# A hybrid encoder block on one core: where the constants are loaded, when the first half's squares are made, and 24 products of the output projection placed elsewhere

## The chip, the core and the metric

The kernel runs on one core of a Trainium2 chip. The metric is the device time of one execution in microseconds (us), as the median of several executions. The engines are named as in the profile: PE (TensorE, matrix products), DVE (VectorE), ACT (ScalarE), POOL (GpSimd), SP (SyncE, which issues most transfers). A "product" is one PE instruction of 128x128 weights by 128x512 columns.

## What is computed

One layer of an encoder block on x of 1024 positions by 1024 channels, in float32: a mixing part (a short gated convolution on one half of the channels, a gated 31-tap convolution with a layernorm on the other) and a gated MLP. Cut to the part of the program that the change touches:

```python
h   = rmsnorm(x, norm_mix_g)
z   = h @ w_in                       # 1024 -> 2560: a_h, a_bg, a_cg, b_val, b_gate, 512 each
y_a = a_bg * dwconv(a_cg * a_h, conv_a_w)                 # 3 taps
u   = dwconv(b_val * sigmoid(b_gate), conv_b_w) + conv_b_b  # 31 taps
y_b = silu(layernorm(u, ln_b_g, ln_b_b))
x   = x + concat(y_a, y_b) @ w_out
# then: h = rmsnorm(x); x = x + (silu(dwconv3(h @ w_gate)) * (h @ w_up)) @ w_down; final rmsnorm
```

## The kernel before

Channels lie on the partitions, positions along the free dimension, in two halves of 512 positions (h = 0 and 1). Each float32 operand of a product is split into a high part (a rounded copy) and a low part (the rest): a tile's k-th step is three products, high x high, high weights x low, low weights x high. ACT makes high parts and DVE or POOL the low ones by a subtraction (`minus`, L93, called from `split`, L131).

**The start (L200 to L282).** The first two tiles of the input projection (gate and value of group 0, weights `w01`) are made step by step as data arrive: `load_h1` makes the high part of x times the norm's gain on ACT (L213) and the low part on DVE (L214), both need the constants `cst`; `split_w01` splits the weights in three pieces, k = 0 to 1, 2 to 3, and 4 to 7 (a copy on DVE, L245, then the subtraction, L93). Each k has six products (L271): 48 of half 0, then 48 of half 1. `sq_h1` makes the squares for the RMS norm: ACT squares (L221, L224), and POOL adds them into `acc1[0]` and the first of half 1 into `acc1[1]`; DVE adds the others of half 1 (L226). `stat_h1` sums an accumulator over the partitions on PE (`total_of`, L185 with the high part and L186 with the low part, which DVE writes as `st`, L93); then follow a square root on ACT (L193) and a reciprocal on DVE (L194). After the two tiles the third begins (`mm_tile`, L166).

x comes in by SP's queue, the weights `w01` by ACT's queue (L241), and the constants by POOL's queue (L251).

**The output projection (L394 to L406 and the loop at the end of the printed code).** It runs over the halves; its operands are eight blocks per half: `yA` (4 blocks, from the gated short convolution, L353 to L367) and `yB` (4 blocks, out of `layernorm`, L374 to L387). For half 0 the first four output tiles (`HEAD`) have their products with k = 0, 1, 2 placed ahead of the layernorm's operands. The last product group of the short convolution, j = 3, ends with L366, which frees its pair of PSUM banks. PSUM tiles of products are taken in pairs from a ring (`psum()`).

A scheduler puts the instructions of each engine in order; the products of the first two tiles stand in the order written, and what is written within `urgent()` is preferred. Each engine then runs its own list strictly in order.

Of the kernel before, what the change touches and what calls it, by code (L numbers as in the profile page):

```python
# [9 lines left out]
AF = mybir.ActivationFunctionType  # L10
# [7 lines left out]
KD = D // P  # L18
D_A = 512
NJ = D_A // P  # L20
# [25 lines left out]
def block_kernel(ctx: ExitStack, tc, xT, win01, win, wout, wgate, wup, wdown, consts, outT):  # L46
    nc = tc.nc
# [56 lines left out]
    def psum():  # L104
        return [ps.tile([P, H], F32, tag="mm", name="mm") for _ in range(2)]
# [112 lines left out]
    def sq_h1(h, k):  # L218
        x = xs[h][:, k, :]
        if k == 0:  # L220
            nc.scalar.activation(acc1[h], x, AF.Square)  # L221
        else:
            sq = scratch("sq")
            nc.scalar.activation(sq[:, :H], x, AF.Square)  # L224
            eng = nc.gpsimd if h == 0 or k < 3 else nc.vector
            eng.tensor_tensor(out=acc1[h], in0=acc1[h], in1=sq[:, :H], op=ALU.add)  # L226
# [13 lines left out]
    def load_w01(a, b):  # L240
        nc.scalar.dma_start(raw01[:, a:b], win01[:, a:b])  # L241

    def split_w01(a, b):
        for i, (hi, lo) in enumerate(w01):
            nc.vector.tensor_copy(hi[:, a:b, :], raw01[:, a:b, i, :])  # L245
            minus(nc.vector, lo[:, a:b, :], raw01[:, a:b, i, :], f32(hi[:, a:b, :]))

    cuts = ((0, 2), (2, 4), (4, 8))
    nc.sync.dma_start(xs[0][:, 0, :], xT[0, :, 0])
    load_w01(*cuts[0])  # L250
    nc.gpsimd.dma_start(cst, consts)  # L251
    nc.sync.dma_start(xs[0][:, 1, :], xT[0, :, 1])
    load_w01(*cuts[1])
    nc.sync.dma_start(xs[0][:, 2:4, :], xT[0, :, 2:4])
# [6 lines left out]
    with tc.manual_schedule(engines={nc.tensor.engine}):  # L261
        for h in range(2):
            for k in range(KD):
                load_h1(h, k)
                if h == 0:
                    for a, b in cuts:
                        if k == a:
                            split_w01(a, b)
                for wz, xz in ((0, 0), (0, 1), (1, 0)):
                    for pt, w in zip((pg, pv), w01):  # L270
                        nc.tensor.matmul(pt[h], w[wz][:, k, :], a1(h, k)[xz], start=k + wz + xz == 0, stop=k == KD - 1 and wz == 1)  # L271
                sq_h1(h, k)
                if h == 1 and k == 3:
                    with urgent():
                        stat_h1(0)

        def late_stat(k):
            if k == 5:
                with urgent():
                    stat_h1(1)  # L280

        pg1 = mm_tile(2, a1, late_stat)  # L282
# [87 lines left out]
    def layernorm(h):  # L370
        cc = [half(cb[j], h) for j in range(NJ)]
        s, std = half(ub[2 * h], 0), half(ub[2 * h], 1)
        q, r = half(ub[2 * h + 1], 0), half(ub[2 * h + 1], 1)
        nc.vector.tensor_tensor(out=s, in0=cc[0], in1=cc[1], op=ALU.add)  # L374
        nc.vector.tensor_tensor(out=s, in0=s, in1=cc[2], op=ALU.add)
        nc.vector.tensor_tensor(out=s, in0=s, in1=cc[3], op=ALU.add)
        m = total(s, nc.vector)
        for j in range(NJ):
            nc.vector.scalar_tensor_tensor(cc[j], m, -1.0 / D_A, cc[j], ALU.mult, ALU.add)
            nc.scalar.activation(q if j == 0 else s, cc[j], AF.Square)  # L380
            if j:
                nc.vector.tensor_tensor(out=q, in0=q, in1=s, op=ALU.add)
        rstd(total(q, nc.vector), std, r, eps_l, D_A)
        for j in range(NJ):
            nc.vector.tensor_tensor(out=cc[j], in0=cc[j], in1=r, op=ALU.mult)
            nc.scalar.activation(cc[j], cc[j], AF.Silu, scale=col(LN_G + j), bias=col(LN_B + j))
            split(cc[j], yB[h][:, j, :], yB[h][:, NJ + j, :], nc.vector)  # L387
# [6 lines left out]
    def out_mm(pt, e, w, h, ks):  # L394
        for k in ks:
            mm3(half(pt, e), w[0][:, k, :], w[1][:, k, :], *y_of(h, k), k == 0, k == KD - 1)
# [45 lines left out]
    for h in range(2):  # L442
        pts, ws = {}, {}

        def start(dt):
            ws[dt] = get(N_IN + 8 * h + dt, 0 if h == 0 and dt < HEAD else 2)
            if dt % 2 == 0:
                pts[dt // 2] = psum()

        head = HEAD if h == 0 else 0  # L450
        for dt in range(head):
            start(dt)
            out_mm(pts[dt // 2], dt % 2, ws[dt], h, range(NJ - 1))
        if h == 0:
            with urgent():
                layernorm(0)
            layernorm(1)
        for dt in range(KD):
            nc.sync.dma_start(half(xr[dt], h), xT[h, :, dt])
            if dt >= head:  # L460
                start(dt)
            out_mm(pts[dt // 2], dt % 2, ws[dt], h, range(NJ - 1 if dt < head else 0, KD))
            out_done(pts[dt // 2], dt, h, accs2[h])
            if h == 1 and dt == 1:
                stat_r2(0, accs2[0])
                norm_x(0, range(KD))
                to_op("B11", 0, 0)
                to_op("B21", 4, 0)
# [675 lines left out]
```

## Time and profile before

| what | value |
|---|---|
| median of 3 runs | 1011.09 us (1010.94 to 1011.56) |
| the profiled execution, its own time | 1009.84 us |
| its span in the trace | 1008.1 us |
| mean granted PE clock | 0.989 of full speed |
| PE busy | 968.3 us, 96% of the span |
| DVE busy | 746.6 us, 74% |
| ACT busy | 446.3 us, 44% |
| POOL busy | 443.8 us, 44% |

The span is the time from the first to the last instruction that the profile records; 1.7 us of the execution lie outside. The profiled execution was 1.25 us faster than the median. All times in the rows below are counted from the start of the span. "Idle before <-X" is time in which the engine stood still ahead of the row, and X is what released it.

### The profile page before, as it was taken

How to read it: one execution, taken by the hardware profiler on the slowest of the kernel's cores; microseconds unless marked ns; L12 is line 12 of the kernel's file. 1: busy time of each engine (PE TensorE's matmuls, PEld its weight loads, DVE VectorE, ACT ScalarE, POOL GpSimd, SP SyncE). 2: the span in 40 equal slices, each digit the busy share in tenths (PEclk: the TensorE clock that was granted, in tenths of full speed). 3: DMA queues.
4: the chain of work that ended last, by engine and by line, in shares of the span. 5: the costliest groups of instructions: out<-in, count | busy, mean ns of one | idle time of the engine just before them, and what ended most of it. 6: DMA issues, size and time to landing. Idle time of an engine off the chain costs nothing.

```text
span 1008.1 us, 11577 instructions
## 1 busy us (share of the span) xinstructions
PE 968.3 (96%) x4202; PEld 792.6 (79%) x4202; DVE 746.6 (74%) x891; ACT 446.3 (44%) x623; POOL 443.8 (44%) x304
## 2 busy tenths in 40 slices
PE   6999999998999999899999999999998999999993
PEld 4888888886888887788888888888786788888883
DVE  7899999999678797754654654654559798786557
ACT  7354421234564456434443443443446353534352
POOL 4189853344853006345244344344325534342006
PEclk8999999999999999999999999999999999999997
DMA  6211111123563204133134133223284763544104
GB/s 255 84 43 63 42 43 62 42 63 105 178 219 128 82 1 149 71 117 135 63 106 145 63 105 132 77 104 120 88 270 140 239 192 98 181 126 125 43 1 167
DMA packets 63178, 112.56 MB, mean 112 GB/s; under 512 B 5488, under 2 KB 26992, under 8 KB 62864
## 3 DMA queue, kind: packets, MB, share of 16 engines
q1 hardware_dynamic: 62640, 110.65, 32.9%
q10 hardware_dynamic: 432, 1.05, 0.3%
q8 instruction: 33, 0.54, 0.2%
q14 instruction: 25, 0.20, 0.1%
q0 software_dynamic: 48, 0.12, 0.0%
HBM read 84.79 MB, written 27.00 MB: 111 GB/s over the span
## 4 chain that ended last, share of the span: by engine, by line
PE 85%; DVE 6%; issue 3%; DMA 2%; POOL 2%; ACT 1%; SPq 0%; POOLq 0%; DVEq 0%; ACTq 0%
PE a L546 28%; PE mm L166 19%; PE c L546 13%; PE b L546 8%; PE mm L152 3%; PE mm L154 3%; PE mm L153 3%; PE a L681 2%; PE mm L271 2%; PE c L681 1%; DMA xd<-x2d 1%; DVE wlo L93 1%; PE y L154 1%; PE y L153 1%; PE y L152 1%
## 5 line engine op out<-in xcount | busy, mean ns | idle before, releaser
L166 PE MATMUL mm<-r,whi 128*128 128x512 f32 x576 | 155.3, 389 | 0.0
L546 PE MATMUL a<-r,whi 128*128 128x512 f32 x472 | 147.4, 393 | 5.9 <-ACT a L531 5.0
L315 DVE SCALAR_TENSOR_TENSOR cv<-u,cst,cv 128x512 f32<-128x512 f32 x203 | 138.9, 749 | 0.7
L166 PEld LDWEIGHTS mm<-r,whi 128*128 128x128 f32 x576 | 108.1, 188 | 22.4
L546 PE MATMUL c<-r,whi 128*128 128x512 f32 x392 | 120.7, 389 | 0.0
L93 POOL TENSOR_TENSOR wlo<-raw,whi 128x1024 fp32r<-128x1024 f32 x30 | 76.7, 2556 | 81.3 <-ACT whi L131 81.1
L131 ACT ACTIVATE whi<-raw 128x1024 fp32r<-128x1024 f32 (+1 forms) x68 | 69.2, 1019 | 95.6 <-PE mm L166 32.9
L546 PEld LDWEIGHTS a<-r,whi 128*128 128x128 f32 x472 | 89.1, 189 | 26.7 <-ACT a L531 5.8
L500 POOL TENSOR_TENSOR s<-raw,s 128x512 f32<-128x512 f32 (+1 forms) x31 | 40.1, 1292 | 139.6 <-DVE wlo L93 118.4
L500 POOL TENSOR_TENSOR s<-up 128x512 f32<-128x512 f32 (+1 forms) x31 | 42.1, 1358 | 133.9 <-DMA up<-wup 117.1
L546 PE MATMUL a<-r,wlo 128*128 128x512 f32 x236 | 93.0, 394 | 2.3 <-DVE wlo L93 2.3
L166 PE MATMUL mm<-r,wlo 128*128 128x512 f32 x288 | 90.2, 389 | 0.0
L131 ACT ACTIVATE whi<-s 128x1024 fp32r<-128x1024 f32 (+1 forms) x52 | 52.2, 1004 | 77.2 <-POOL s L500 59.3
L546 PEld LDWEIGHTS c<-r,whi 128*128 128x128 f32 x392 | 73.6, 188 | 15.3
L93 DVE TENSOR_TENSOR wlo<-s,whi 128x1024 fp32r<-128x1024 f32 (+1 forms) x52 | 65.0, 1249 | 27.7 <-ACT whi L131 27.7
L90 POOL TENSOR_TENSOR t<-t 128x512 f32<-128x512 f32 x36 | 53.8, 1506 | 66.7 <-DVE t L603 66.7
L624 DVE TENSOR_TENSOR t<-a,c 128x512 f32<-128x512 f32 x40 | 27.4, 686 | 69.9 <-issue 37.3
L546 PE MATMUL c<-r,wlo 128*128 128x512 f32 x196 | 76.2, 389 | 0.0
L531 ACT ACTIVATE a<-a 128x512 f32<-128x512 f32 x76 | 45.1, 593 | 65.2 <-PE a L546 62.5
L546 PE MATMUL a<-r,ahi 128*128 128x512 f32 x224 | 70.5, 396 | 1.1 <-DVE xd L862 1.1
L546 PE MATMUL b<-r,whi 128*128 128x512 f32 x232 | 71.4, 389 | 0.0
L131 ACT ACTIVATE r<-r 128x512 fp32r<-128x512 f32 x71 | 43.7, 628 | 52.4 <-DMA r<-ydT 23.6
(209 smaller groups left out, 2114.9 us busy)
## 6 DMA issues: line engine op xcount, KB each, us to landing
raw<-wgate SPq DMA_DIRECT2D x22, 512.0 KB, 4.7
up<-wup SPq DMA_DIRECT2D x20, 512.0 KB, 3.3
raw<-win SPq DMA_DIRECT2D x18, 512.0 KB, 3.3
ydT<-t SPq DMA_DIRECT2D x36, 256.0 KB, 2.0
r<-ydT SPq DMA_DIRECT2D x36, 256.0 KB, 3.3
raw<-wout SPq DMA_DIRECT2D x16, 512.0 KB, 3.4
ydB<-t SPq DMA_DIRECT2D x27, 256.0 KB, 2.0
r<-ydB SPq DMA_DIRECT2D x27, 256.0 KB, 4.4
```

The source lines that it names most:

```text
L90: nc.gpsimd.tensor_tensor(out=out, in0=a, in1=b, op=op)
L93: eng.tensor_tensor(out=out, in0=a, in1=b, op=ALU.subtract)
L131: nc.scalar.activation(hi, y, AF.Copy)
L152: nc.tensor.matmul(out, whi, hi, start=first, stop=False)
L153: nc.tensor.matmul(out, whi, lo, start=False, stop=False)
L154: nc.tensor.matmul(out, wlo, hi, start=False, stop=last)
L166: nc.tensor.matmul(outs[h], w, a[h][z], start=s0, stop=s1)
L315: nc.vector.scalar_tensor_tensor(fin if k == KC - 1 else acc, src, w, acc, ALU.mult, ALU.add)
L500: self.eng.tensor_tensor(out=self.t[:, i * self.w : (i + 1) * self.w], in0=a, in1=b, op=op)
L531: nc.scalar.activation(t, b, AF.Copy)
L546: nc.tensor.matmul(out, w[wz][:, k, :], x[xz], start=first and k + wz + xz == 0, stop=k == n - 1 and wz == 1, skip_group_check=not first)
L681: nc.tensor.matmul(out, w[wz][:, k, :], xz, start=first and k == 0 and wz == 0 and xz is hi, stop=not first and k == 3 and wz == 1)
```

## The change

The constants' transfer goes from POOL's queue to the head of ACT's queue, ahead of the weights. The high parts of the third piece of `w01` (k = 4 to 7) are made by ACT instead of DVE. The squares of half 0 are issued four steps later, the last four during half 1, and the first total stands after k = 5 of half 1 instead of k = 3. In the output projection the four head tiles' products of k = 3 and twelve products of half 1's first output tile (with half 0's weights, into a pair of banks `first1`) are written ahead of the loop over the output tiles.

```diff
@@ -242,13 +242,16 @@
 
     def split_w01(a, b):
         for i, (hi, lo) in enumerate(w01):
-            nc.vector.tensor_copy(hi[:, a:b, :], raw01[:, a:b, i, :])
+            if a < 4:
+                nc.vector.tensor_copy(hi[:, a:b, :], raw01[:, a:b, i, :])
+            else:
+                nc.scalar.activation(hi[:, a:b, :], raw01[:, a:b, i, :], AF.Copy)
             minus(nc.vector, lo[:, a:b, :], raw01[:, a:b, i, :], f32(hi[:, a:b, :]))
 
     cuts = ((0, 2), (2, 4), (4, 8))
     nc.sync.dma_start(xs[0][:, 0, :], xT[0, :, 0])
+    nc.scalar.dma_start(cst, consts)
     load_w01(*cuts[0])
-    nc.gpsimd.dma_start(cst, consts)
     nc.sync.dma_start(xs[0][:, 1, :], xT[0, :, 1])
     load_w01(*cuts[1])
     nc.sync.dma_start(xs[0][:, 2:4, :], xT[0, :, 2:4])
@@ -269,8 +272,13 @@
                 for wz, xz in ((0, 0), (0, 1), (1, 0)):
                     for pt, w in zip((pg, pv), w01):
                         nc.tensor.matmul(pt[h], w[wz][:, k, :], a1(h, k)[xz], start=k + wz + xz == 0, stop=k == KD - 1 and wz == 1)
-                sq_h1(h, k)
-                if h == 1 and k == 3:
+                if h == 0 and k >= 4:
+                    sq_h1(0, k - 4)
+                if h == 1:
+                    if k < 4:
+                        sq_h1(0, k + 4)
+                    sq_h1(1, k)
+                if h == 1 and k == 5:
                     with urgent():
                         stat_h1(0)
 
@@ -444,10 +452,12 @@
 
         def start(dt):
             ws[dt] = get(N_IN + 8 * h + dt, 0 if h == 0 and dt < HEAD else 2)
-            if dt % 2 == 0:
+            if dt % 2 == 0 and dt // 2 not in pts:
                 pts[dt // 2] = psum()
 
         head = HEAD if h == 0 else 0
+        if h == 1:
+            pts[0] = first1
         for dt in range(head):
             start(dt)
             out_mm(pts[dt // 2], dt % 2, ws[dt], h, range(NJ - 1))
@@ -455,11 +465,15 @@
             with urgent():
                 layernorm(0)
             layernorm(1)
+            for dt in range(head):
+                out_mm(pts[dt // 2], dt % 2, ws[dt], h, [NJ - 1])
+            first1 = psum()
+            out_mm(first1, 0, ws[0], 1, range(NJ))
         for dt in range(KD):
             nc.sync.dma_start(half(xr[dt], h), xT[h, :, dt])
             if dt >= head:
                 start(dt)
-            out_mm(pts[dt // 2], dt % 2, ws[dt], h, range(NJ - 1 if dt < head else 0, KD))
+            out_mm(pts[dt // 2], dt % 2, ws[dt], h, range(NJ if dt < head or (h, dt) == (1, 0) else 0, KD))
             out_done(pts[dt // 2], dt, h, accs2[h])
             if h == 1 and dt == 1:
                 stat_r2(0, accs2[0])
```

DVE's list from the third piece of the weights to the first reciprocal. r_95 and r_97 are the low parts of x of half 0 and half 1, acc_118 and acc_119 the two halves' accumulators, whi_120 and whi_122 the high parts of `w01`. Before:

```order
L245 CAST whi_120<-rr 128x512
L245 CAST whi_122<-rr 128x512
L214 SCALAR_TENSOR_TENSOR r_95<-c,cst,r_94 128x512
L93 TENSOR_TENSOR wlo_121<-rr,whi_120 128x512
L93 TENSOR_TENSOR wlo_123<-rr,whi_122 128x512
L214 SCALAR_TENSOR_TENSOR r_95<-c,cst,r_94 128x512 x4
L214 SCALAR_TENSOR_TENSOR r_97<-u,cst,r_96 128x512 x4
L226 TENSOR_TENSOR acc_119<-acc_119,sq 128x512
L93 TENSOR_TENSOR st<-acc_118,st 128x512
L214 SCALAR_TENSOR_TENSOR r_97<-u,cst,r_96 128x512 x4
L93 TENSOR_TENSOR wlo<-raw,whi 128x1024 x2
L194 RECIPROCAL rr<-std 128x512
```

And with the change:

```order
L214 SCALAR_TENSOR_TENSOR r_95<-c,cst,r_94 128x512 x4
L93 TENSOR_TENSOR wlo_121<-rr,whi_120 128x512
L93 TENSOR_TENSOR wlo_123<-rr,whi_122 128x512
L214 SCALAR_TENSOR_TENSOR r_95<-c,cst,r_94 128x512 x2
L214 SCALAR_TENSOR_TENSOR r_97<-u,cst,r_96 128x512 x4
L226 TENSOR_TENSOR acc_119<-acc_119,sq 128x512
L214 SCALAR_TENSOR_TENSOR r_97<-u,cst,r_96 128x512 x4
L226 TENSOR_TENSOR acc_119<-acc_119,sq 128x512
L93 TENSOR_TENSOR wlo<-raw,whi 128x1024
L226 TENSOR_TENSOR acc_119<-acc_119,sq 128x512
L93 TENSOR_TENSOR wlo<-raw,whi 128x1024
L93 TENSOR_TENSOR st<-acc_118,st 128x512
```

The two copies are gone, the low parts of x for k = 2 to 5 stand in one row ahead of the weights' third piece, and `st` of the first total has moved from behind one addition to behind three additions, four low parts and two splits of 128x1024 weights (the second and third input tiles' weights come from `raw`).

POOL's list at the start, before:

```order
L251 DMA cst<-consts 128x238
L300 MEMSET u 128x16
L226 ISA
L226 TENSOR_TENSOR acc_118<-acc_118,sq 128x512 x7
L299 MEMSET u 128x16
L226 TENSOR_TENSOR acc_119<-acc_119,sq 128x512 x2
```

And with the change:

```order
L308 MEMSET u 128x16
L226 ISA
L226 TENSOR_TENSOR acc_118<-acc_118,sq 128x512 x5
L307 MEMSET u 128x16
L226 TENSOR_TENSOR acc_119<-acc_119,sq 128x512
L226 TENSOR_TENSOR acc_118<-acc_118,sq 128x512
L226 TENSOR_TENSOR acc_119<-acc_119,sq 128x512
L307 MEMSET u 128x16
L226 TENSOR_TENSOR acc_118<-acc_118,sq 128x512
```

Two of half 0's seven additions now stand behind the MEMSET, which writes into the region of `u` that holds half 1's x and so follows DVE's low part of half 1's k = 0.

PE's list where the output projection begins. r4_98 is yA of half 0, r5_99 yA of half 1; mm_1801, mm_1802, mm_1827 and mm_1828 are the four head tiles, whi_1667 the first head tile's weights, mm_1953 the new pair `first1`. Numbers at the waits are semaphores. Before:

```order
L152 MATMUL mm_1828<-r4_98,whi_1840 128x512 [waits DVE_49,Activation_49]
L153 MATMUL mm_1828<-r4_98,whi_1840 128x512
L152 MATMUL mm_1801<-r4_98,whi_1667 128x512 [waits Activation_49]
L152 MATMUL mm_1802<-r4_98,whi_1730 128x512
L152 MATMUL mm_1827<-r4_98,whi_1823 128x512
L154 MATMUL mm_1828<-r4_98,wlo_1841 128x512 [waits Pool_49]
```

And with the change:

```order
L152 MATMUL mm_1828<-r4_98,whi_1840 128x512 [waits DVE_49,Activation_49]
L153 MATMUL mm_1828<-r4_98,whi_1840 128x512
L152 MATMUL mm_1953<-r5_99,whi_1667 128x512 [waits DVE_49]
L153 MATMUL mm_1953<-r5_99,whi_1667 128x512
L154 MATMUL mm_1953<-r5_99,wlo_1668 128x512
```

These three rows of mm_1953 are its k = 0; six more for k = 1 and 2 follow, and only then the row of mm_1801 that waits for ACT. So nine products have come between the last product that runs before PE's wait and the product that waits. The first of the nine waits for DVE, which frees the pair of banks of the short convolution's last product group in L366.

## Rows read from the trace of the kernel before

**Rows 1.** The page: the span, its first part (busy time, share and instructions of each engine), and the shares of the chain of work that ended last, by engine.

```profile
span 1008.1 us, 11577 instructions
...
PE 968.3 (96%) x4202; PEld 792.6 (79%) x4202; DVE 746.6 (74%) x891; ACT 446.3 (44%) x623; POOL 443.8 (44%) x304
...
PE 85%; DVE 6%; issue 3%; DMA 2%; POOL 2%; ACT 1%; SPq 0%; POOLq 0%; DVEq 0%; ACTq 0%
```

**Rows 2.** What PE waited for from 0 to 420 us: line, releaser, us in total, times, longest.

```profile
PE mm L271 <- DVE r L214: 4.3, 3, 2.9
PE mm L152 <- ACT r L131: 3.5, 1, 3.5
PE a L546 <- ACT a L531: 3.1, 1, 3.1
PE mm L271 <- ACT r L213: 2.8, 1, 2.8
```

**Rows 3.** The chain of work that ended last, pieces in order of time: start, us, what.

```profile
1.26 6.18 DMA cst<-consts
...
47.86 163.23 PE mm L166 x720
...
245.94 0.64 ACT r L131
246.62 0.98 PE mm L152 x3
```

**Rows 4.** Transfers issued in the first 30 us: queue, count, KB each, median us from issue to landing.

```profile
rr<-win ACTq DMA_DIRECT2D x2, 256.0 KB, 5.0
...
cst<-consts POOLq DMA_DIRECT2D x1, 119.0 KB, 6.2
```

**Rows 5.** ACT at the start, two rows: start, us, line, operation, idle before and its releaser.

```profile
5.07 0.63 ACT L221 ACTIVATE acc<-c 128x512 f32<-128x512 f32 x1 [2.38 <-DMA c<-xT]
...
9.70 0.72 ACT L213 ACTIVATE r<-c,cst 128x512 fp32r<-128x512 f32 x1 [0.38 <-DMA c<-xT]
```

**Rows 6.** DVE from 9 to 35 us, start and us of each group of instructions.

```profile
12.81 1.77 DVE L214 SCALAR_TENSOR_TENSOR r<-c,cst,r 128x512 fp32r<-128x512 f32 x1
14.50 2.93 DVE L245 CAST whi<-rr 128x512 fp32r<-128x512 f32 x2
17.36 1.75 DVE L214 SCALAR_TENSOR_TENSOR r<-c,cst,r 128x512 fp32r<-128x512 f32 x1
19.03 2.37 DVE L93 TENSOR_TENSOR wlo<-rr,whi 128x512 fp32r<-128x512 f32 x2
21.33 2.73 DVE L214 SCALAR_TENSOR_TENSOR r<-c,cst,r 128x512 fp32r<-128x512 f32 x4
...
29.30 0.68 DVE L93 TENSOR_TENSOR st<-acc,st 128x512 fp32r<-128x512 f32 x1
...
32.56 2.34 DVE L93 TENSOR_TENSOR wlo<-raw,whi 128x1024 fp32r<-128x1024 f32 x2
```

**Rows 7.** POOL's additions of squares at the start.

```profile
9.40 10.85 POOL L226 TENSOR_TENSOR acc<-acc,sq 128x512 f32<-128x512 f32 x7 [7.31 <-ACT sq L224]
...
24.89 3.34 POOL L226 TENSOR_TENSOR acc<-acc,sq 128x512 f32<-128x512 f32 x2
```

**Rows 8.** PE from 19 to 40 us: the last two waits of the start, the second product of the first total, and the start of the third tile.

```profile
19.16 0.82 PE L271 MATMUL mm<-r,whi 128*128 128x512 f32 x2 [2.88 <-DVE r L214]
...
22.12 1.16 PE L271 MATMUL mm<-r,whi 128*128 128x512 f32 x2 [0.43 <-DVE r L214]
...
33.37 0.39 PE L186 MATMUL total<-st,ones_r 128*128 128x512 f32 x1
...
39.06 1.07 PE L166 MATMUL mm<-r,whi 128*128 128x512 f32 x4
```

**Rows 9.** DVE's reciprocal for the second half's norm.

```profile
48.68 3.35 DVE L194 RECIPROCAL rr<-std 128x512 f32<-128x512 f32 x1 [2.65 <-ACT std L193]
```

**Rows 10.** Stretches of the span: from:to, us, busy time (instructions) of PE, PEld, DVE, ACT and POOL, the granted PE clock (1.00 is the full 2.4 GHz, 0.50 is 1.2 GHz), DMA share, GB/s.

```profile
19.70:23.00 3.30, 2.87 (x7) 1.77 (x6) 3.30 (x5) 3.30 (x7) 0.56 (x1) 0.50 0.00 0
23.10:240.00 216.90, 216.90 (x957) 179.49 (x956) 206.07 (x286) 84.16 (x113) 121.33 (x77) 1.00 0.18 58
241.50:248.30 6.80, 3.30 (x15) 2.41 (x14) 6.73 (x8) 1.23 (x2) 4.25 (x3) 1.00 0.46 137
...
408.80:412.10 3.30, 3.30 (x10) 2.52 (x9) 3.26 (x2) 0.00 (x0) 2.49 (x2) 0.50 0.00 0
```

**Rows 11.** PE behind its wait at 405 us: the first row after it, and the tenth product.

```profile
408.35 0.87 PE L546 MATMUL a<-r,whi 128*128 128x512 f32 x2 [3.12 <-ACT a L531]
...
412.01 0.71 PE L546 MATMUL a<-r,whi 128*128 128x512 f32 x2
```

**Rows 12.** DVE where the output projection begins: the last two low parts of yB of half 0, and the first half's product of the short convolution's last group.

```profile
239.63 5.01 DVE L93 TENSOR_TENSOR r<-c,r 128x512 fp32r<-128x512 f32 x2
...
245.22 0.68 DVE L366 TENSOR_TENSOR y<-mm,y 128x512 f32<-128x512 f32 x1
```

**Rows 13.** The same stretch on POOL: a split of the output projection's weights.

```profile
241.28 2.82 POOL L93 TENSOR_TENSOR wlo<-raw,whi 128x1024 fp32r<-128x1024 f32 x1
```

**Rows 14.** DVE's last low part of yB of half 1, and PE's products that read it.

```profile
287.53 2.29 DVE L93 TENSOR_TENSOR r<-c,r 128x512 fp32r<-128x512 f32 x1
...
290.62 0.62 PE L153 MATMUL mm<-r,whi 128*128 128x512 f32 x2
```

## The prediction

> **What bounds the kernel now.** I began with the page. PE is busy for 96% of the span, and 85% of the chain that ended last is PE's own work [rows 1]. No product is removed by the change, so it can only save time in which PE stands still or runs at half clock. The view of PE's waits lists where that is in the first 420 us, the stretch that the change touches: 4.3 us for low parts of x that DVE makes at the start, 2.8 us for the first high part, 3.5 us once in the output projection, and 3.1 us at 405 us, which the change doesn't touch [rows 2]. The chain names the sources: at the very start the constants, which land 6.18 us after their issue, and at 246 us ACT's high part of the short convolution's output [rows 3]. Last I looked at what lies between the two places. From the end of the start to 240 us PE works without a pause at full clock [rows 10], 720 products in 163.23 us [rows 3], so one product costs 0.2267 us. DVE waits there for what PE produces (its reciprocal at 48.68 us stood 2.65 us idle for a total that PE had to reach) [rows 9]. Therefore PE's start carries through: each microsecond by which the third tile begins earlier than at 39.06 us [rows 8] is worth a microsecond at the end, as long as nothing later takes it back.
>
> **The constants.** Before, they land at 7.44 us [rows 3] and the first high part on ACT follows. At the head of ACT's queue they should land near 5 us, as the weights issued there do, 5.0 us after their issue [rows 4]; the weights go out one issue later. PE may so begin 2 us earlier. I count this as nothing: the third step needs x for k = 2, whose transfer lands when ACT takes it at 9.70 us, after an idle time for that transfer [rows 5]. That is unchanged, so both orders restart there. The same cover hides a later landing too; if x for k = 2 came at once, the 2 us would count in full.
>
> **The start on DVE.** Before, the low part of k = 2 begins only at 12.81 us, since four DVE instructions ahead of it share the time with POOL's additions. The rows show what that costs: POOL's seven additions run from 9.40 to 20.25 us, 1.55 each [rows 7], and in that stretch a low part takes 1.75 to 1.77 us, a copy 1.47, while from 21.33 us four low parts take 2.73, 0.68 each [rows 6]. Each DVE instruction waits for the addition in flight; I call that a hold, and one costs 1.75 - 0.68 = about 1.05 us.
>
> I laid the new lists out by hand with these durations. The second piece of the weights is split before k = 2 arrives. Its high part ends at 10.4, so DVE makes k = 2 at 10.5, k = 3 at 11.1, k = 4 at 12.8 and, held, k = 5 from 13.5 to 15.3. The two copies of the third piece take ACT 0.63 each [rows 5], done at 15.5, ahead of their use. DVE's two subtractions of that piece are both held by POOL's fourth and fifth additions: they end at 17.0 and 18.7. Before they ended at 19.03 + 2.37 = 21.40, and PE's last wait of the start ended at 22.12 [rows 8]. The low part at 18.7 is the operand of product 30 of the 96. From there to the third tile are 67 products and the two of the total, 69 x 0.2267 = 15.6 us: 34.3 instead of 39.06. That alone would be 4.8 us, and it is the upper bound of this term.
>
> **The wait that comes instead.** The second product of the first total (L186) needs the low part `st` on DVE. Before, `st` was made at 29.30 us [rows 6] and PE came to it at 33.37 [rows 8], 3.4 us later. Now both sides move against each other. PE comes 55 products after 18.7, near 31.4. On DVE, k = 6, 7 and half 1's k = 0 end at 20.7; then POOL's list is free to go past its MEMSET and makes three additions in turn, at 1.67 each [rows 7], to 25.9. Half 1's k = 1 ends at 21.3, k = 2 and 3, held, at 24.7; the first addition of DVE's own stands behind POOL's third and ends at 26.6; k = 4, held by POOL's last addition, ends at 28.3; k = 5 to 7 at 30.3; the second addition at 30.9; the first split of 1024 columns (1.17 each [rows 6]) at 32.0; the third addition at 32.7; the second split at 33.9; and `st`, 0.68, at 34.5. So PE waits near 3.1 us, to 34.6. Twelve products and L186 follow, 13 x 0.2267 = 2.95: the third tile begins at 37.55. **First term: 39.06 - 37.55 = 1.5 us faster.** One hold more makes it 0.45, two make it -0.6; with no wait left it is 4.8. I keep 1.5, since the holds that I count are those of the rows.
>
> Late next is the square root and the reciprocal behind the total: they come 1.3 us later than before (34.6 against 33.37), but what reads the first norm is the gate of tile one, which has the third tile (48 products, 10.9 us) as cover. POOL's squares of half 1 and DVE's remaining work are hidden under the same.
>
> **PE's clock.** A wait of that length may cost more. In the kernel before, the wait of 2.88 us that ended at 19.16 [rows 8] is followed by 3.30 us at granted clock 0.50, and the one of 3.12 us that ended at 408.35 too [rows 10, 11]; the wait of 3.50 us in the output projection [rows 2] is not: the clock stays 1.00 [rows 10]. What a fall costs can be read at 408.35: the tenth product began at 412.01, nine products in 3.66 us instead of 2.04, so 1.6 us. The Trainium skill says the same of the cause (TensorE: Matmul & The Clock Gate, section "What's actually happening"): "the default state is throttled, and activity releases the throttle". By that rule a new wait endangers the gain; if the fall were certain and whole, this kernel's sum would be 1.5 + 0.65 - 1.6 = 0.55 us; the trace agrees in two of the three waits of this length. I take that it falls, since two of three did, and that a third of the slow stretch lies still under the wait or beside it: **second term: 1.05 us slower**, bounds 0 and 1.6.
>
> **The output projection.** Before, PE runs out of products with operands at 243.1 and starts again at 246.62, when ACT has made the first high part of the last group's product, which DVE forms in L366 from 245.22 to 245.90 [rows 3, 12]. The change puts nine products into that gap, 9 x 0.2267 = 2.04 us. But the bank pair that they write is freed by that same L366: they wait for DVE until 245.90, and can begin near 245.97 instead of 246.62. **Third term: 0.65 us faster**, not 2.04. The upper bound is 2.04, if the pair were free; the lower is nothing. The other moved products (k = 3, and three of half 1 that have to wait for the second half's high part) change places with others that had their operands: yB's low parts end at 239.63 + 5.01 = 244.64 [rows 12], before PE's restart, so no wait is there to fill. Holding the bank pair of half 1's tile early costs nothing, as the pair was idle. The splits of the weights for the later output tiles come nearer to their use, by those 24 products (24 x 0.2267 = 5.4 us): one split on POOL takes 2.82 [rows 13], so without that cover each would cost up to 2.8; I see about 5 us of cover left and count nothing.
>
> **Sum:** 1.5 - 1.05 + 0.65 = 1.1 us. The profiled execution took 1009.84 us; minus 1.1 is 1008.7, and as it was 1.25 below the median, I expect a median of 1010.0 us. A measurement of this kernel can tell about 0.2%, 2.0 us, from no change.
>
> **The rivals.**
>
> *No fall of the clock, or one hold fewer.* The third wait before left the clock at 1.00. Then the gain is 1.5 + 0.65 = 2.15, with a hold fewer up to 3.6: 1007.5 to 1008.95. Against it stand the two falls. Chance 0.23.
>
> *No wait at the total.* If POOL's additions hold DVE far less in the new order, `st` is ready when PE comes: 4.8 + 0.65 = 5.45, 1005.6. Against it: three splits and additions stand ahead of `st` whatever the holds do. Chance 0.08.
>
> *The gain is eaten whole.* With two holds more, or if half 0's last two additions come still later, the first total takes all, and the output projection stays as it was: -0.6 to 0.5 of gain, 1010.6 to 1011.7. The change then doesn't do what it seems to. Chance 0.14.
>
> *Slower, by a new wait at the end of half 1's layernorm.* DVE's last low part of yB ends at 287.53 + 2.29 = 289.82 and PE's products that read it begin at 290.62 and 290.84 [rows 14], a slack of 1.0. With nine products done earlier PE comes 0.65 sooner relative to DVE, and I see 0.4 of slack left. It decides from 0.4 on: if one split of POOL's (up to 2.82 [rows 13]) holds that chain, PE stalls by 2.0, giving 1.1 - 2.0, so 1012.0; with a fall of the clock behind it, 1.6 more: 1013.6. For it speaks that the 2.29 us of that row is a held instruction already; against it that POOL's list is unchanged there. Chance 0.12.
>
> **How the numbers follow.** The forecast case holds 0.43, with times of 1009 to 1010.9, its likeliest 1010.0. Faster by over 0.2% means below 1009.07: the first two rivals, 0.31, and the forecast's fast edge, 0.06. Slower by over 0.2% is above 1013.1: the last rival's worse part and a rest, 0.08. Between is 0.55. The range that leaves out no more than 0.2 reaches from 1007.0 (leaving out most of the second rival) to 1012.5 (leaving out the clock's fall in the last).
>
> **What the profile of the changed kernel would show.** The first step is right if the third piece's subtractions end near 18.7 us and no wait over 2 us stands at L274 after 10 us. The second: a PE wait of 2 to 4 us at L186 for DVE's `st`, and the third tile near 37.5. The third: a stretch of granted clock 0.50 right after it, or not. The fourth: in the output projection a wait that ends with DVE's product (L374), and nine products of half 1 straight behind it, at 245.97 less the start's net gain. The prediction is wrong if `st` comes before PE, if the clock is other than taken, if the pair is free earlier, or if a wait near 290 us appears that was not there.

## The result and the profile after

The changed kernel took 1014.28 us (median of 6 runs, 1012.92 to 1015.58) where the kernel before took 1011.33 beside it: ratio 1.0028, interval 1.0015 to 1.0041. It is 3 us slower; 1010.0 was forecast. Ratios, here and below, are of executions in the fast state: one execution of e1, 1394.68 us at a mean granted clock of 0.654, is left out of its ratio. The profiled execution took 1012.92 us, 3.1 more than the profiled one of before.

The page of after, lines of its first and fourth part, against [rows 1]:

```profile
span 1011.1 us, 11583 instructions
...
PE 970.1 (96%) x4202; PEld 792.2 (78%) x4202; DVE 746.4 (74%) x889; ACT 447.2 (44%) x625; POOL 441.3 (44%) x303
...
PE 80%; DVE 6%; issue 3%; ACT 3%; DMA 2%; POOL 2%; SPq 0%; POOLq 0%; DVEq 0%; ACTq 0%
```

The work is the same; the chain holds 80% of PE's own work instead of 85%, and 3% of ACT's instead of 1%. What PE waited for from 0 to 420 us in after (line, releaser, us in total, times, longest), against [rows 2]:

```profile
PE total L186 <- DVE st L93: 4.3, 2, 2.8
...
PE mm L152 <- DVE y L374: 2.8, 1, 2.8
...
PE mm L274 <- DVE r L214: 1.7, 2, 1.0
...
PE mm L274 <- DVE whi L246: 1.4, 1, 1.4
PE mm L153 <- DVE r L93: 0.8, 2, 0.6
PE mm L274 <- DVE wlo L93: 0.5, 1, 0.5
```

The 4.3 us for low parts of x at the start shrank to 1.7, the 2.8 us ahead of the first product to 1.4 (it now waits for the weights' copy, L246), and the 3.5 us in the output projection to 2.8. New are 0.5 us for the weights' third piece, the total's second product, once at the start (2.8) and once much later (1.5), and L153, products that read yB.

PE at three places: the last wait of the start, the total and the third tile (against [rows 8]), and the restart in the output projection.

```profile
18.45 1.10 PE L274 MATMUL mm<-r,wlo 128*128 128x512 f32 x2 [0.53 <-DVE wlo L93]
...
34.84 0.50 PE L186 MATMUL total<-st,ones_r 128*128 128x512 f32 x1 [2.77 <-DVE st L93]
...
37.91 1.07 PE L166 MATMUL mm<-r,whi 128*128 128x512 f32 x4
...
244.77 0.79 PE L152 MATMUL mm<-r,whi 128*128 128x512 f32 x1 [2.80 <-DVE y L374]
```

Third tile: 37.91 against 39.06, 1.15 us earlier. Restart: 244.77 against 246.62, 1.85 earlier, so the output projection's wait gave 0.70. But the first product of the feed-forward part (36 products with the norm's operands) begins at 331.98 in after and at 328.74 in before: between these places 5.09 us were lost. Two stretches hold them. First the clock: stretches from:to with PE's busy time (products), PEld, DVE, ACT, POOL, the granted clock, DMA share and GB/s, behind the wait at the total and behind the restart:

```profile
34.80:38.20 3.40, 3.36 (x15) 2.80 (x16) 2.04 (x1) 2.50 (x4) 0.11 (x1) 1.00 0.64 180
...
244.80:248.10 3.30, 3.30 (x8) 2.62 (x9) 3.19 (x5) 1.17 (x2) 2.52 (x2) 0.50 0.62 227
```

Behind the total nothing fell; behind the restart the clock was at half, and the ninth product began at 248.25, 3.48 us after the first, against 1.97 in before (248.59 - 246.62): 1.5 us lost. Then the waits between 285 and 305 us, where before has none:

```profile
290.56 0.50 PE L153 MATMUL mm<-r,whi 128*128 128x512 f32 x1 [0.58 <-DVE r L93]
...
292.25 0.50 PE L153 MATMUL mm<-r,whi 128*128 128x512 f32 x1 [0.27 <-DVE r L93]
...
301.47 0.50 PE L186 MATMUL total<-st,ones_r 128*128 128x512 f32 x1 [1.53 <-DVE st L93]
```

The view counts 2.4 us there, and the starts of neighbouring products 3.1. The whole stretch from the ninth product to the feed-forward part takes 331.98 - 248.25 = 83.73 in after and 328.74 - 248.59 = 80.15 in before, 3.6 more. Sum: -1.15 - 0.70 + 1.5 + 3.6 = +3.25 us.

That is the sum of one pair of executions, and the clock's 1.5 us in it is not to be charged to the change. Three kernels below have the output projection of before (e1, e5 and the one called total last), and in all three the clock fell behind the same restart: from 243 to 252 us it is 0.81, 0.81 and 0.65, against 0.81 in after and 1.00 in before. So the profile of before is the odd one. Against e1, whose clock fell as in after, the stretch from the third tile to the feed-forward part is 294.07 - 291.14 = 2.9 us longer: that is what the moved products cost, the 0.70 that they gained taken off.

Why those waits? ACT's high part of the next weights waits for PE to free a weight buffer. The row in before, then in after:

```profile
252.43 1.06 ACT L131 ACTIVATE whi<-raw 128x1024 fp32r<-128x1024 f32 x1 [5.27 <-PE mm L153]
```

```profile
256.17 1.06 ACT L131 ACTIVATE whi<-raw 128x1024 fp32r<-128x1024 f32 x1 [4.85 <-PE mm L153]
```

Counted from the third tile this is 213.4 before and 218.3 after, 4.9 us later. The order of PE's products says why: the last product that reads the first head tile's high weights was number 53 of the output projection and is now number 71, since the moved products stand ahead of it. 18 x 0.2267 = 4.1, plus the clock's 1.5, less the 0.70 of the earlier restart: 4.9.

The later splits are late with it, by 4.4 to 7.0 us up to the ninth. The layernorm of half 1 is not late from its beginning: the first DVE instruction behind its first total (`c<-total`) begins 221.0 us behind the third tile in after and 220.8 in before. PE finishes its second total 1.9 us late (235.5 against 233.6), and the square root behind that total is 4.4 us late (238.0 against 233.6): in both lists it stands behind the fifth split on ACT. That split and the root in before, then in after:

```profile
268.58 1.04 ACT L131 ACTIVATE whi<-raw 128x1024 fp32r<-128x1024 f32 x1
...
272.68 0.69 ACT L193 ACTIVATE u<-total,eps_l 128x512 f32<-128x512 f32 x1 [0.40 <-PE total L186]
```

```profile
273.05 1.06 ACT L131 ACTIVATE whi<-raw 128x1024 fp32r<-128x1024 f32 x1 [2.85 <-DMA raw<-wout]
...
275.94 0.69 ACT L193 ACTIVATE u<-total,eps_l 128x512 f32<-128x512 f32 x1
```

Before, ACT waits for PE's total. In after PE has the total done at 273.44, while ACT is still at the split, whose weights came late. DVE's last low part of yB then ends 254.3 us behind the third tile instead of 250.8. The wait at the third total has another last link. SP, ACT and DVE in after:

```profile
286.56 5.99 SPq L473 DMA_DIRECT2D c<-xT  x3
292.64 0.38 SPq L127 DMA_DIRECT2D raw<-wout  x1
```

```profile
297.34 1.06 ACT L131 ACTIVATE whi<-raw 128x1024 fp32r<-128x1024 f32 x1 [3.88 <-DMA raw<-wout]
298.31 0.61 ACT L179 ACTIVATE st<-acc 128x512 fp32r<-128x512 f32 x1
```

The third of SP's loads of x (L473) writes over a block that DVE's last low part of yB reads, and that ended at 292.20; the weights' load stands behind it on the same queue and lands at 297.3; ACT's high part of these weights waits for it, and the high part `st` of the norm's total stands behind that on ACT. PE reaches the total and waits until 301.47. Before, ACT made this `st` at 291.00, ahead of the weights.

### The profile page after: what moved, and what is told of

It reads as the page before. It is cut to its first block, busy times and chain, and to the rows that moved or that the text cites. A ratio compares the mean times of both kernels' runs of the same rounds, so it can differ in the third digit from the quotient of the medians.

```text
span 1011.1 us, 11583 instructions
## 1 busy us (share of the span) xinstructions
PE 970.1 (96%) x4202; PEld 792.2 (78%) x4202; DVE 746.4 (74%) x889; ACT 447.2 (44%) x625; POOL 441.3 (44%) x303
## 4 chain that ended last, share of the span: by engine, by line
PE 80%; DVE 6%; issue 3%; ACT 3%; DMA 2%; POOL 2%; SPq 0%; POOLq 0%; DVEq 0%; ACTq 0%
PE a L560 28%; PE mm L166 19%; PE c L560 13%; PE b L560 8%; PE a L695 2%; PE mm L152 1%; PE mm L154 1%; PE mm L153 1%; PE c L695 1%; DVE r L93 1%; DMA raw<-wout 1%; DMA xd<-x2d 1%; PE y L153 1%; PE y L154 1%; PE y L152 1%
## 5 line engine op out<-in xcount | busy, mean ns | idle before, releaser
L93 POOL TENSOR_TENSOR wlo<-raw,whi 128x1024 fp32r<-128x1024 f32 x30 | 74.0, 2465 | 84.9 <-ACT whi L131 84.6
```

The lines of the kernel that those rows point to most:

```text
L93: eng.tensor_tensor(out=out, in0=a, in1=b, op=ALU.subtract)
```

## The experiments

All are compared with the kernel before in the same sessions. What each edit left in the profile, in us from the start of the span: third tile, first product of the feed-forward part (FF), and the stretch between them. Per row the stretch speaks of the output projection alone, the third tile of the start alone, each in one execution.

| kernel | third tile | FF | stretch | ratio to before (interval) |
|---|---|---|---|---|
| before | 39.06 | 328.74 | 289.68 | |
| changed | 37.91 | 331.98 | 294.07 | 1.0028 (1.0015 to 1.0041) |
| e1, start only | 39.47 | 330.61 | 291.14 | 0.9991 (0.9980 to 1.0002) |
| e2, output projection only | 38.41 | 332.76 | 294.35 | 1.0031 (1.0019 to 1.0042) |
| e3, without half 1's products | 39.59 | 332.55 | 292.96 | 1.0002 (0.9992 to 1.0012) |
| e4, without k = 3 | 37.69 | 329.52 | 291.83 | 0.9997 (0.9986 to 1.0007) |
| e5, squares as before, start only | 37.12 | 328.37 | 291.25 | 0.9983 (0.9973 to 0.9993) |
| total last, start only | 35.85 | 328.31 | 292.46 | 0.9964 (0.9953 to 0.9976) |
| the same, PE's wait filled | 35.94 | 325.63 | 289.69 | 0.9953 (0.9942 to 0.9965) |
| total last, yB's products first | 36.57 | 324.29 | 287.72 | 0.9936 (0.9922 to 0.9950) |
| yB's products first alone | 40.96 | 330.75 | 289.79 | 0.9991 (0.9979 to 1.0003) |
| total last, yB first, three tiles | 35.98 | 321.84 | 285.86 | 0.9925 (0.9905 to 0.9945) |

How far one execution's third tile can be trusted, the three rows with the start of before show: 39.06, 38.41 (e2) and 40.96 (yB's products first alone), with a granted clock from 13 to 40 us of 0.94, 1.00 and 0.87. PE's wait is the same in all three. The row of before stands in [rows 8]; e2 and the third:

```profile
18.95 0.73 PE L271 MATMUL mm<-r,whi 128*128 128x512 f32 x2 [2.88 <-DVE r L214]
```

```profile
19.17 0.73 PE L271 MATMUL mm<-r,whi 128*128 128x512 f32 x2 [2.87 <-DVE r L214]
```

With the changed start it is 37.91 at clock 1.00, and 39.47 (e1), 39.59 (e3) and 37.69 (e4) at 0.94. At clock 1.00 the changed start gains 0.5 us (38.41 against 37.91); more than half of the 1.15 us above comes with the lower clock of before.

### The two halves of the change apart

Start only: the output projection of before in the changed kernel.

```diff
...
-            for dt in range(head):
-                out_mm(pts[dt // 2], dt % 2, ws[dt], h, [NJ - 1])
-            first1 = psum()
-            out_mm(first1, 0, ws[0], 1, range(NJ))
...
-            out_mm(pts[dt // 2], dt % 2, ws[dt], h, range(NJ if dt < head or (h, dt) == (1, 0) else 0, KD))
+            out_mm(pts[dt // 2], dt % 2, ws[dt], h, range(NJ - 1 if dt < head else 0, KD))
```

> The changed kernel with the output projection written as before; only the start is changed. Theory 1 (the loss is made in the output projection: its first weight buffers come free 18 products later, and the second half's layernorm and weight splits slip behind them): the third tile begins near 37.9 us as in the changed kernel, PE waits once near 245 us for ACT and nowhere between 285 and 305, and the median is 1.0 to 1.5 us below the kernel before. Rival (the earlier start itself disturbs the later order, so that the waits near 290 and 301 us come from it): the waits near 290 and 301 us are there, and the median is 1 us or more above the kernel before.

Output projection only: the start of before in the changed kernel.

```diff
...
-    nc.scalar.dma_start(cst, consts)
     load_w01(*cuts[0])
+    nc.gpsimd.dma_start(cst, consts)
...
+                sq_h1(h, k)
+                if h == 1 and k == 3:
...
```

> The kernel before with only the output projection's 24 products moved; the start is that of before. Theory 1: PE waits for DVE's low parts of yB near 291 us and for the low part of the third total near 302 us, together 2.5 to 3.5 us, and the median is 2.5 to 5 us above the kernel before, the upper end if the granted clock falls behind the wait at 246 us. Rival (the start is at fault): no wait between 285 and 305 us, and a median 0.3 to 1 us below the kernel before.

Start only: no wait between 285 and 305 us, ratio 0.9991. Output projection only: 1.0031, with 1.5 us of wait at L186 and 1.1 at L153 in that stretch. The rival falls: the loss is the output projection's, 3.1 us by the ratio. The start's gain was 0.9 us by the ratio, and its interval (0.9980 to 1.0002) does not leave out no gain; in this profile the third tile began at 39.47, no gain at all. The granted clock of this kernel behind its wait at the total, and behind the restart in the output projection:

```profile
34.90:38.20 3.30, 3.30 (x9) 2.58 (x10) 2.09 (x1) 1.72 (x3) 0.11 (x1) 0.54 0.57 182
247.10:250.40 3.30, 3.30 (x8) 2.61 (x9) 3.16 (x5) 0.48 (x1) 2.48 (x2) 0.53 0.44 178
```

Here both waits, 2.75 and 3.51 us long, cost the clock; in the changed kernel the first, 2.77 long, did not. 39.47 against 37.91 is 1.56 us for the one fall, 291.14 against 289.68 is 1.46 for the other.

### The output projection's two moves apart

```diff
...
-            first1 = psum()
-            out_mm(first1, 0, ws[0], 1, range(NJ))
...
```

> The changed kernel without the twelve products of half 1's first tile; only the four head tiles' products of k = 3 stay ahead. The first weight buffer then comes free 6 products later than before instead of 18. Theory 1: the second half's layernorm is late by about a third as much, the PE waits between 285 and 305 us shrink below 1 us in all, and the median is 0.5 to 1.5 us below the kernel before. Rival (any move of the k = 3 products upsets the order on ACT and SyncE): waits of 2 us or more stay there and the median is above the kernel before.

```diff
-            for dt in range(head):
-                out_mm(pts[dt // 2], dt % 2, ws[dt], h, [NJ - 1])
...
```

> The changed kernel with the head tiles' products of k = 3 left where they were; only the twelve products of half 1's first tile are moved. The first weight buffer comes free 11 products later than before, against 18 in the changed kernel and 6 with k = 3 moved alone. Theory 1 (what counts is how late the weight buffers come free): PE waits near 290 to 302 us for 1.5 to 3 us in all, and the median is 0.5 to 2.5 us above the kernel before. Rival (only the order of k = 3 matters): no such waits, and the median is at or below the kernel before.

The first weight split after the head came 216.0 us behind the third tile with k = 3 alone and 216.8 with half 1's products alone; before 213.4, after 218.3. Worked out: 6 x 0.2267 + 1.5 for the clock = 2.9 later (measured 2.6), and 11 x 0.2267 + 1.5 - 0.65 = 3.3 (measured 3.4). So the buffers explain when the splits begin. They do not alone explain PE's wait: k = 3 alone waits 1.7 us at L153, half 1's products alone wait 0.7 us in all, at L186, though its buffers come free later. The engines' lists differ between the two, and which place in them decides is open. Neither half costs what both do together: 1.0002 and 0.9997, beside 1.0028 for both and 0.9991 for neither (e1). Both expectations missed. Of k = 3 alone under 1 us of waits and 0.5 to 1.5 us of gain were expected; it had 1.7 us of waits and 0.2 of loss. Of half 1's products alone 1.5 to 3 us of waits and 0.5 to 2.5 us of loss were expected; they had 0.7 us of waits and, by the ratio, 0.3 of gain, nearer to that rival than to the theory.

### Where the start's gain went

The total behind k = 7 of half 1, output projection as before:

```diff
-                if h == 1 and k == 5:
+                if h == 1 and k == 7:
...
```

> The start of the changed kernel with the first total behind k = 7 of half 1 instead of k = 5, the output projection as before. If the wait at the first total is what eats the start's gain, twelve products fill it: the wait falls from 2.8 us to below 1 us, the third tile begins near 35.7 us, and the median is 3 to 3.6 us below the kernel before. If the later reciprocal delays the first gates instead, a new PE wait stands before 60 us and the gain stays below 2 us.

PE at the total and the third tile in that kernel:

```profile
34.45 0.40 PE L185 MATMUL total<-st,ones_r 128*128 128x512 f32 x1
35.52 0.50 PE L186 MATMUL total<-st,ones_r 128*128 128x512 f32 x1 [0.67 <-DVE st L93]
35.85 1.09 PE L166 MATMUL mm<-r,whi 128*128 128x512 f32 x4
```

The wait fell from 2.77 to 0.67, the third tile began 3.2 us earlier than before, and the ratio is 0.9964, where e1 with the total behind k = 5 has 0.9991: the wait at the total was what ate most of the gain. No wait came in its place before 60 us.

The other way round, squares and total as before, with the constants and the copies moved:

```diff
-                if h == 0 and k >= 4:
-                    sq_h1(0, k - 4)
-                if h == 1:
-                    if k < 4:
-                        sq_h1(0, k + 4)
-                    sq_h1(1, k)
-                if h == 1 and k == 5:
+                sq_h1(h, k)
+                if h == 1 and k == 3:
...
```

> Only the constants' queue and the copies on ACT are changed; squares, first total and output projection are as before. It asks what the later squares are worth. If the later squares are what lets DVE finish sooner, the additions on POOL hold DVE as before, the third piece of the weights is split 1 to 2 us later than in the changed kernel (near 20 us), but the first total finds its operand ready, so that the third tile begins at 36 to 37.5 us. If the squares' place does nothing for DVE, the split ends near 18.5 us, no wait stands at the total, and the third tile begins near 34.5 us. By either the median is 1.5 to 4.5 us below the kernel before, better than the start of the changed kernel.

```profile
20.71 1.10 PE L274 MATMUL mm<-r,wlo 128*128 128x512 f32 x2 [0.53 <-DVE wlo L93]
...
31.43 0.39 PE L186 MATMUL total<-st,ones_r 128*128 128x512 f32 x1
...
37.12 1.07 PE L166 MATMUL mm<-r,whi 128*128 128x512 f32 x4
```

The third piece is split 2.3 us later than in the changed kernel (20.71 against 18.45), but the total waits for nothing, and the third tile begins 0.8 us earlier than there. So later squares do free DVE, as both the prediction and the change have it, and the total's place then takes more than that back. Ratio 0.9983, beside 0.9991 for e1; the two intervals overlap.

### The clock and the wait in the output projection

The total-last kernel with 14 products that nobody reads, in PE's wait:

```diff
+            fl = psm.tile([P, H], F32, tag="sm", name="fl")
+            for _ in range(14):
+                nc.tensor.matmul(fl, ones_r, yA[0][:, 2, :], start=True, stop=True)
```

> The kernel with the first total last (start as changed, total behind k = 7, output projection as before), and in addition 14 products whose result nobody reads, placed where PE waits in the output projection; they take 14 x 0.2267 = 3.2 us of a wait of 3.5 us. If the granted clock falls because PE stands still there, it stays at 1.00, and the stretch from PE's restart to the first product of the feed-forward part takes 82.1 us as in the kernel before instead of 84.9: median 1.3 to 2.8 us below the same kernel without the fill. If the loss there is of another kind, the two kernels have the same time.

The granted clock behind the restart, without the fill and with it:

```profile
243.50:246.80 3.30, 3.30 (x8) 2.62 (x9) 3.16 (x5) 0.49 (x1) 2.48 (x2) 0.50 0.44 176
246.90:250.20 3.30, 3.30 (x11) 2.54 (x10) 1.69 (x3) 0.00 (x0) 0.00 (x0) 0.62 0.00 0
```

```profile
243.50:246.80 3.30, 3.25 (x14) 2.72 (x15) 3.16 (x5) 0.60 (x1) 2.55 (x2) 1.00 0.48 185
```

The restart is at the same place (243.44 and 243.55), but the stretch from it to the feed-forward part takes 84.87 without and 82.08 with the fill, as long as in before (82.12). So PE's standing still is what costs the clock, here 2.8 us in one execution and 1.1 us by the ratios, whose intervals overlap; 1.3 to 2.8 were expected. The other profiles bear it out: in the four in which this wait is filled (this one and the three below) the clock from 243 to 252 us is 1.00, and of the eight in which it is not, only before has 1.00 there.

Real work in the same place: yB's k = 4 and 5 ahead of k = 3.

```diff
+            for dt in range(head):
+                out_mm(pts[dt // 2], dt % 2, ws[dt], h, [4, 5])
...
```

> The kernel with the first total last, and in the output projection the head tiles' products of k = 4 and 5 of half 0 (operands from the layernorm, ready from 239 us) ahead of those of k = 3, whose operand PE waits for. They use the same four weights and free no buffer later in time. If PE's wait of 3.5 us is time lost, it vanishes and the median is 3 to 5 us below the same kernel without this. If the second half's layernorm has only the 1 us of slack that I read, PE waits 2 to 3 us near 287 us for DVE's low parts of yB instead, and the median is 0 to 2 us below.

> The kernel before, with only the order of the head tiles' products changed: k = 4 and 5 of half 0 ahead of k = 3; the start and everything else as before. With the start of the total-last kernel this order took 2.7 us off its time. If that gain is the output projection's own, it is here too: no wait near 243 us, one of 1 to 2 us near 290 us, and a median 1.5 to 3.5 us below the kernel before. If it depends on the earlier start (the granted clock fell for twice as long in that kernel without it), the gain here is below 1.5 us.

With the total last: 0.9936, beside 0.9964 without this order. All that PE waited for from 235 to 335 us:

```profile
PE mm L153 <- DVE r L93: 1.6, 1, 1.6
```

On the kernel before alone: 0.9991 (not clear of no change), a stretch of 289.79, and of 3.5 us of wait filled, 3.2 come back:

```profile
PE mm L153 <- DVE r L93: 3.2, 2, 1.7
```

So both readings held in part. The wait of 3.5 us can be filled, but PE then runs into DVE's last low parts of yB of half 1, which have about the 1 us of slack that was read. Why the earlier start leaves 1.6 of it rather than 3.2 was not settled.

The slack itself: three output tiles of half 1 instead of two with their yA products ahead.

```diff
-        head = HEAD if h == 0 else 0
+        head = HEAD if h == 0 else 3
...
```

> The total-last kernel with k = 4 and 5 ahead of k = 3, and besides that three instead of two output tiles of half 1 have their twelve products with yA ahead of the first product that reads yB of half 1. That gives DVE twelve products, 2.7 us, more until its last low parts of yB are needed, and holds three weight buffers longer. If the wait of 1.6 us near 287 us is the layernorm's lateness alone, it vanishes and the median is 1 to 2 us below the kernel with two tiles ahead, 7 to 8 below the kernel before. If the weight buffers that come free later cost as much as in the changed kernel, a wait stands behind it and the median is the same or higher.

```profile
PE total L186 <- DVE st L93: 0.2, 1, 0.2
```

That is all that PE waits from 235 to 335 us; the stretch is 285.86, 3.8 below before, and the ratio 0.9925, 1004.26 us against 1011.57: faster than both kernels. Three weight buffers are held longer here, and the trace shows no cost of it: the first split stands 213.4 us behind the third tile, as in before.

## Why the prediction was wrong

**The start: right in kind, too large.** Forecast 1.5 us; the pair of profiles has 1.15, profiles of equal clock 0.5, and e1 0.9 by its ratio. The wait that comes instead was there, at L186, 2.77 long where 3.1 was worked out, ending at 34.84 (34.6). That it ate most of the start's gain is shown by the total-last kernel.

The holds stood elsewhere than laid out. DVE in after:

```profile
11.96 5.83 DVE L214 SCALAR_TENSOR_TENSOR r<-c,cst,r 128x512 fp32r<-128x512 f32 x4
17.72 1.28 DVE L93 TENSOR_TENSOR wlo<-rr,whi 128x512 fp32r<-128x512 f32 x2
```

The four low parts were held (1.46 each, end 17.8 instead of 15.3), the two subtractions were not (0.64 each). They ended at 19.0 instead of 18.7: two errors that nearly cancel, so that this time came out by luck. The constants' step was misjudged too: I took the landing of x for k = 2 as unchanged at 9.70. ACT's row in after:

```profile
8.26 1.34 ACT L213 ACTIVATE r<-c,cst 128x512 fp32r<-128x512 f32 x2 [0.87 <-DMA c<-xT]
```

In all nine kernels with the constants on ACT's queue ACT takes that x at 8.26 to 8.76 us, in the three without at 9.49 to 9.71. So x for k = 2, the cover under which the constants' gain was to vanish, itself came about 1.2 us earlier; DVE, held by POOL, used it up: k = 2 to 5 began at 11.96, not at 10.5.

**The clock: right price, wrong place.** The price of 1.6 us for a whole fall held (1.46 to 1.56 for one fall, 2.8 once). I charged one fall to the total's wait. In after none came there, and one behind the restart in the output projection, which I had taken as safe because it was so in the one profile of before. In the eight profiles in which PE stands there for 2.8 to 3.5 us (before, after, e1 to e5, total last) the clock fell in seven; at the total's wait of 2.8 us it fell in e1 and e3 and not in after. Behind the wait of 2.88 us at the start, which the prediction counts as a fall, it fell in before and in the third kernel with that start, and not in e2. One profile could not tell that. Of the slow products at a kernel's start the Trainium skill says that their number is run-variable (TensorE: Matmul & The Clock Gate, section "What's actually happening"); what varies here, in line with it, is the clock behind one and the same wait, 0.94, 1.00 and 0.87 from 13 to 40 us in the three profiles with the start of before. So a term for the clock belongs to an execution more than to this change, and neither the 1.05 of the forecast nor the 1.5 us of the pair of profiles can be put down to it.

**The bank pair: right.** 0.65 forecast, 0.70 measured: the nine products waited for L374, and 0.65 of the 2.04 us was to be had.

**The step that failed: the weights behind the moved products.** I wrote that their splits come nearer to their use by 24 products and that "about 5 us of cover" remains, so "count nothing". The products were counted, and the release was not followed: moving 18 products ahead of the first head tile's end frees its buffer 18 products later. The next split moves by 4.9 us (3.4 against e1, whose clock fell at the same place: 218.3 and 214.8 behind the third tile), the layernorm's second total comes 1.9 us late and its root, held on ACT by the fifth split, 4.4, and DVE's last low part of yB ends 3.5 us later, while PE has no more work than before until it needs it. The term was put at nothing; it measured 3.6 us behind the restart, and output projection only costs 3.1 us by its ratio. That the moved products make the loss, and that the buffers set when the splits begin, is shown by the experiments. The way from a late split to PE's waits is read from the trace of after: no run has a fifth buffer, or the root ahead of the split, and the two moves apart do not wait in the order in which their buffers come free. That part stays open.

**The slower rival: right place, wrong mechanism and too little chance.** I named the wait at DVE's last low part of yB with 0.4 us of slack, for a stall of 2.0, if a split on POOL held DVE. The stall came (0.58 and 0.27 by the view) with the layernorm's late root, together with the wait at the third total, which I had not seen. It got 0.12.

## What to carry to other kernels

Before moving products ahead, ask what they hold: for each buffer, find the last product that reads it in the new order and who waits for its release; a release that is 18 products late here delayed a square root some 30 us further on, behind a split in ACT's list. A product that fills a wait should read only weights that stay anyway: k = 4 and 5 of the same tiles filled 3.5 us and left the first split where it was (213.4 us behind the third tile), the moved products gave 0.7 and cost 3.6. And when an operand is made faster, move what waits behind it too: with the total two steps later the same start gave 3.6 us by the ratio instead of 0.9. Last, a difference of 1 or 2 us between two single profiles can be the clock's: look at the granted clock of both before putting it down to the edit.

## What the runs showed of the hardware

A wait of PE of some 3 us costs the granted clock in some executions and not in others of nearly the same instruction order, about 1.5 us each time, and 2.8 where the fall lasted for two stretches of 3.3 us (0.50, then 0.62). Products in the wait, useless or not, kept it at 1.00 in four profiles of four. DVE's instructions beside POOL's additions took 1.46 us each in after and 1.75 to 1.77 in before instead of 0.68, but the held ones were not those that the hand-made order gave. With the constants' 119 KB on ACT's queue instead of POOL's, x for k = 2, on SP's queue, landed some 1.2 us sooner (8.26 to 8.76 us in nine profiles against 9.49 to 9.71 in three); why is not shown.
